# Two-layer diffusion backbone: the first two projection items of a chunk issued in turns, and the second layer's modulation moved to later items

## The chip, the cores and the metric

One NeuronCore of one Trainium2 chip. The metric is the device time of one execution in microseconds; three runs of the kernel before are shown by their median. One profiled execution is read in detail. The engines are TensorE (PE, its weight loads PEld), VectorE (DVE), ScalarE (ACT), GpSimd (POOL) and SyncE (SP), which here issues the DMA transfers.

## The reference

Two layers, each: RMS norm with a modulation computed from a condition vector, one input projection whose columns feed three mixers (latent attention, grouped attention, a convolution module), a gate on each, one output projection, and a residual.

```python
shift, scale, gate = split(silu(c) @ w_mod + b_mod, 3)
h = rms_norm(x, norm_w) * (1 + scale) + shift
p = h @ w_in                               # 2048 tokens x 1024, and 256 context tokens likewise
y = concat([o_mla, o_gqa, o_conv]) * silu(p[..., OFF_GATE:])
x_new = x + gate * (y @ w_out)
```

After the second layer comes a final RMS norm. Everything is float32.

## The kernel before, in words

The kernel alternates three calls of `projections(l)` (l = 0 and 1 for the layers, 2 for the end stage, which has the last output projection only) with two calls of `attention`. The change lies in `projections`.

**The work of a projection stage** is a list of *items* (L517 on): one weight tile of 128 output columns times one chunk of tokens. Chunks 0 to 3 have 512 tokens, chunk 4 is the context with 256. Kind "o" is the output projection of the layer before, kind "i" the input projection; the first layer has 105 items, the second 128, the end stage 32. An item takes 24 matmuls: for each of 8 slices k of the contraction the three products wh·xh, wh·xl and wl·xh, since weight and operand are each split into a rounded part (h) and a remainder (l). They add up in one PSUM bank of `mm` (two banks; three in the end stage).

**Weights.** `w_loads` brings raw tiles into two buffers `wraw`; `w_splits` turns raw weight j into `wset[j % 2]`, ACT rounding it to wh and POOL subtracting to wl. It may do so only after the last item that uses weight j − 2 (the `after(("item", w_last[j - 2]))` in it).

**Operands.** `x_prep(c)` makes chunk c's operands for kind "i", slice by slice: DVE scales a loaded tile of x by the modulation and the norm's bank, ACT adds the shift and rounds into xh, DVE subtracts into xl; then slice k counts as there. They stand in `big`: chunks 0 and 2 in `big2`, chunks 1 and 3 in `big0`, the context in `big1`. `y_k` does the like for kind "o". `stats` computes a chunk's norm, `post` and `out_post` take an item's result out of PSUM, `mod_part(m, part, start)` computes a part of layer m's modulation: w_mod tiles of 256 KB, in groups of four matmuls that run side by side in four strips of the array, and then transposes. It waits for item `start` to begin (`at(start)` looks at `at_item`).

**What sets the order.** A planner in the kernel, which runs when it is built: `Sched` holds generators with priorities, `Clock` a model of when each engine is free and each tile readable, and `Sched.run` lets the generators issue whatever the model holds ready. Each engine then carries out its instructions in the order in which they were issued. `mains` (L585), with priority 9, issues the items one after another: per slice it yields until the weights and the slice are ready, and after every second slice it yields once more. So whatever changes in the pace of `mains` changes the order on DVE, ACT, POOL and SP as well.

Of the kernel before, what the change touches and what calls it, by code (L numbers as in the profile page):

```python
# [22 lines left out]
CH = [(0, 512), (512, 512), (1024, 512), (1536, 512), (2048, 256)]  # L23
EPS = 1e-6
KD = D // 128
# [22 lines left out]
INF = float("inf")  # L48
# [240 lines left out]
def hybrid_dit(ctx: ExitStack, tc: tile.TileContext, I: dict, out: bass.AP):  # L289
    nc = tc.nc  # L290
    clk = Clock()
    V, A, G, T = (Engine(clk, n, e) for n, e in
                  (("DVE", nc.vector), ("ACT", nc.scalar), ("POOL", nc.gpsimd), ("PE", nc.tensor)))
# [37 lines left out]
    wset = [[const.tile([128, KD, 128], F32R, name=f"w{s}{i}") for s in "hl"] for i in range(2)]  # L331
# [96 lines left out]
    def q_parts(z, u, q):  # L428

        h, c = u  # L430
        W = CH[c][1]
        if h < MH:
# [6 lines left out]
        for e in (0, 64):  # L439
            parts += [(q[i][e:e + 64, 0:W], n[i]) for i in range(2)]  # L440
            if h < MH:
                parts += [(q[2][e + 32 * i:e + 32 * i + 32, 0:W], src[i, 64:96, :]) for i in range(2)]
                parts.append((q[3][e:e + 32, 0:W], src[0, 64:96, :]))
        return [(o.bitcast(F32), i) for o, i in parts]

    def m_parts(u, q, row):
        W = CH[u[1]][1]
        return [(q[3][e:e + 1, 0:W].bitcast(F32), row.unsqueeze(0)) for e in (32, 96)]

    def projections(l):  # L450
# [5 lines left out]
        sch = Sched(clk, S)  # L456
        load, store = sch.load, sch.store
        done = set()
        at_item = [0]
        open_ = [True]  # L460

        def after(what):
            return lambda: 0.0 if what in done else INF

        def at(n):
            return lambda: 0.0 if at_item[0] >= n else INF
# [35 lines left out]
        items = []  # L502
# [21 lines left out]
        w_last, x_first, x_last = {}, {}, {}  # L524
# [49 lines left out]
        def operand(who):  # L574
            t = big[hold[who]]
            if who[1] == 4:
                t = t[:, 0].rearrange("p (s k) (e w) -> p s (k e) w", s=2, e=2)
            return t[:, 0], t[:, 1]

        def freed(who):  # L580
            if before[who] is None:
                return after("S1") if who == ("o", 1) else None
            return after(("item", before[who]))

        def mains():  # L585
            for n, (j, c, kind, what) in enumerate(items):
                at_item[0] = n
                W = CH[c][1]
                ps = yield from mm.take()
                if kind == "o":  # L590
                    sch.add(0, out_post(n, c, what, ps[:, 0:W]))
                wh, wl = wset[j % 2]
                yield after(("w", j))
                xh, xl = operand((kind, c))
                ops = ((wh, xh), (wh, xl)) if what == "kr" else ((wh, xh), (wh, xl), (wl, xh))
                i = 0
                for k in range(KD):
                    yield [wh, wl, after((kind, c, k))]
                    for a, b in ops:
                        T.matmul(out=ps[:, 0:W], lhsT=a[:, k, :], rhs=b[:, k, 0:W],  # L600
                                 start=(i == 0), stop=(i == len(ops) * KD - 1))
                        i += 1
                    if k % 2:
                        yield
                done.add(("item", n))
                if kind == "i":
                    sch.add(0, post(what, c, ps[:, 0:W]))
            at_item[0] = len(items)
            open_[0] = False

# [678 lines left out]
        def rest_y():  # L1289
            yield from all_y([(c, k) for c in ochunks[2:] for k in range(KD)])  # L1290
            open_lanes[0] = False
# [13 lines left out]
        with ExitStack() as es:  # L1305
            wk = es.enter_context(tc.tile_pool(name=f"wk{l}", bufs=1, reuse_waits="tile"))
            pb = es.enter_context(tc.tile_pool(name=f"pb{l}", bufs=1, space=PSUM, reuse_waits="tile"))
            new = [wk.tile([128, 512], F32, name=f"sb{l}_{i}") for i in range(NSLOT + (10 if end else 0))]
            if first:
                sb = Slots(clk, lent)  # L1310
            sb.extend(new)
            sr = Slots(clk, [] if end else [big[1][:, 1, k, :] for k in range(1, KD)]
                       + [wk.tile([128, 512], F32R, name=f"sr{l}_{i}") for i in range(NSLOTR)])
            wn = Slots(clk, [wk.tile([128, 512 + 2 * HALO], F32, name=f"wn{l}_{i}") for i in range(0 if end else 2)])
            mm = Slots(clk, [pb.tile([128, 512], F32, name=f"mm{l}_{i}") for i in range(3 if end else NMM)])
            aux = Slots(clk, [pb.tile([128, 512], F32, name=f"aux{l}_{i}") for i in range(5 if end else 8 - NMM)])
            if not end:
                sw = es.enter_context(tc.tile_pool(name=f"sw{l}", bufs=1, reuse_waits="tile"))
                p = pars[l]
                qn, kvn, gkn, dww, dwb, lnw, lnb, pwb = p.qn, p.kvn, p.gkn, p.dww, p.dwb, p.lnw, p.lnb, p.pwb  # L1320
                gqs = p.gqn
                V.tensor_scalar(out=gqs, in0=p.gqn, scalar1=0.125, scalar2=None, op0=ALU.mult)
                uv_h = sw.tile([128, 384], F32R, name=f"uv_h{l}")
                uv_l = sw.tile([128, 384], F32R, name=f"uv_l{l}")

            sch.add(9, mains())
            if first:
                sch.add(1, w_loads())
                sch.add(1, w_splits())
            else:  # L1330
                sch.add(2, rest_y())
                for _ in range(LANES_P):
                    sch.add(2, runner(lanes, open_lanes))
            if not end:
                if first:
                    sch.add(2, stats(0, True, None))
                    sch.add(2, mod_part(0, 0, 0))
                    sch.add(3, stats(1, KEEP1, after(("raw", 1)) if AFTW else after("w_mod")))
                    sch.add(3, stats(4, False, at(1)))
                    sch.add(3, stats(2, False, at(20)))  # L1340
                    sch.add(3, stats(3, False, at(30)))
                    sch.add(6, mod_part(0, 1, 14), 2000)
                    sch.add(6, mod_part(1, 0, 50), 2000)
                    sch.add(6, mod_part(1, 1, 70), 2000)
                for c in (0, 1, 4, 2, 3):
                    sch.add(2, x_prep(c))
                sch.add(6, small_weights(n_out + 2), 3000)
                sch.add(3, runner(heavy, open_), 6000)
                for _ in range(2):
                    sch.add(4, runner(light, open_), 5000)  # L1350
                for _ in range(2):
                    sch.add(5, conv_run(), CLIM)
                sch.add(5, first_unit(), 6000)
            sch.run()
# [405 lines left out]
```

## Time and profile before

| | us |
|---|---|
| median of 3 runs | 3965.18 (3965.15 to 3965.5) |
| profiled execution | 3964.66 |
| its span, first to last instruction | 3962.8 |
| PE busy | 3838.4 (97%) |
| DVE, POOL, ACT busy | 2699.1, 2487.7, 1869.5 |

The profile's times count from the start of the span; all steps run through helpers on line L160, so that tiles, not lines, tell the work apart. PE busy is the time with at least one matmul under way; the granted clock is TensorE's, 1.00 for full speed, and a matmul at 0.50 takes twice as long.

### The profile page before, as it was taken

What the parts mean: (1) busy time and instruction counts of PE and PEld (TensorE: products, weight loads), DVE (VectorE), ACT (ScalarE), POOL (GpSimd) and SP (SyncE); (2) the same over time, 40 slices, a digit from 0 to 9 for tenths busy, and PEclk for the clock granted to TensorE, in tenths of its full rate; (3) what the DMA queues carried; (4) which work ended last, traced back from release to release, by engine and by line L of the source; (5) the groups of instructions that cost most, each with busy time, mean ns of one, the idle gap of its engine ahead of it and who ended that gap; (6) DMA issues with size and microseconds to landing.
All of it is one profiled execution on the core that took longest, in us unless ns stands there. A gap on an engine that the chain in (4) does not pass through costs nothing. (4 is left out here: it accounts for less than half of the span.)

```text
span 3962.8 us, 60573 instructions
## 1 busy us (share of the span) xinstructions
PE 3838.4 (97%) x22674; PEld 2645.0 (67%) x22674; DVE 2699.1 (68%) x4017; ACT 1869.5 (47%) x2461; POOL 2487.7 (63%) x1277
## 2 busy tenths in 40 slices
PE   7999999899999999999999999999999999999998
PEld 4888677555556666665778887775655666666576
DVE  5545379688888776677434645887888877666743
ACT  5555376444444444444435645654444444444442
POOL 3452164377777777778445424547888788888844
PEclk9999999899999999999999999999999999999999
DMA  6456654411212332212654463543121133222264
GB/s 214 159 174 200 193 164 148 109 36 37 61 36 65 88 77 66 70 55 79 233 180 136 159 200 126 182 137 75 37 59 28 48 78 77 64 63 69 79 216 148
DMA packets 314712, 438.44 MB, mean 111 GB/s; under 512 B 78625, under 2 KB 149102, under 8 KB 314418
## 3 DMA queue, kind: packets, MB, share of 16 engines
q1 hardware_dynamic: 314418, 434.56, 36.9%
q8 instruction: 179, 2.93, 0.3%
q14 instruction: 115, 0.94, 0.1%
HBM read 304.94 MB, written 121.07 MB: 108 GB/s over the span
## 5 line engine op out<-in xcount | busy, mean ns | idle before, releaser
L160 PE MATMUL mm<-big,wh 128*128 128x512 f32 (+1 forms) x4240 | 1282.6, 388 | 34.1 <-DVE big L160 18.0
L160 POOL TENSOR_TENSOR acc<-acc,p 128x1024 f32<-128x1024 f32 x478 | 1174.2, 2456 | 207.5 <-DVE p L160 130.4
L160 DVE TENSOR_REDUCE mx<-m 128x1 f32<-128x512 f32 (+2 forms) x1716 | 1079.1, 680 | 223.4 <-PE m L160 216.1
L160 ACT ACTIVATE p<-s 128x1024 f32<-128x1024 f32 (+1 forms) x682 | 695.0, 1020 | 746.3 <-PE s L160 701.0
L160 PEld LDWEIGHTS mm<-big,wh 128*128 128x128 f32 x4240 | 782.7, 190 | 234.7 <-issue 53.7
L160 PE MATMUL s<-qh,big 64*128 64x512 f32 (+1 forms) x3504 | 794.4, 408 | 1.0 <-DVE n L160 0.4
L160 PE MATMUL mm<-big,wl 128*128 128x512 f32 (+1 forms) x2040 | 775.8, 380 | 2.9 <-POOL wl L160 2.9
L160 POOL TENSOR_TENSOR wl<-wraw,wh 128x1024 fp32r<-128x1024 f32 x132 | 317.9, 2410 | 614.9 <-ACT wh L160 581.1
L160 PE MATMUL o<-p,big 128*64 128x512 f32 (+1 forms) x2728 | 655.8, 599 | 3.3 <-DVE n L160 3.1
L160 PE MATMUL m<-big,qh 64*128 64x512 f32 (+1 forms) x2304 | 476.1, 360 | 32.7 <-DVE mx L160 24.0
L160 PEld LDWEIGHTS s<-qh,big 64*128 64x128 f32 x3504 | 401.9, 186 | 135.2 <-issue 88.1
L160 PEld LDWEIGHTS mm<-big,wl 128*128 128x128 f32 x2040 | 388.2, 190 | 76.1 <-POOL wl L160 4.6
L160 PEld LDWEIGHTS o<-p,big 128*64 128x64 f32 x2728 | 188.9, 138 | 361.5 <-issue 350.1
L160 PE MATMUL s<-ql,big 64*128 64x512 f32 (+1 forms) x1752 | 390.8, 390 | 0.0
L160 POOL TENSOR_TENSOR acc<-acc,wraw 128x1024 f32<-128x1024 f32 x142 | 346.3, 2439 | 48.7 <-DVE wraw L160 32.9
L160 PEld LDWEIGHTS m<-big,qh 64*128 64x128 f32 x2304 | 298.4, 188 | 113.8 <-DVE mx L160 64.5
L160 DVE SCALAR_TENSOR_TENSOR aux<-wn,par,aux 128x512 f32<-128x512 f32 (+1 forms) x396 | 259.7, 718 | 99.7 <-ACT aux L160 63.8
L160 POOL TENSOR_TENSOR sb<-sb,sb 128x512 f32<-128x512 f32 (+2 forms) x151 | 182.8, 1220 | 204.6 <-ACT sb L160 160.3
L160 ACT ACTIVATE wraw<-s 128x1024 f32<-128x1024 f32 (+1 forms) x194 | 198.2, 1022 | 175.5 <-PE s L160 163.9
L160 DVE SCALAR_TENSOR_TENSOR aux<-aux,sb 128x512 f32<-128x512 f32 (+1 forms) x198 | 129.4, 654 | 147.8 <-ACT sb L160 143.1
L160 PEld LDWEIGHTS s<-ql,big 64*128 64x128 f32 x1752 | 207.9, 187 | 14.7
L160 PE MATMUL s<-qd,zm 33*128 33x512 f32 (+1 forms) x876 | 208.0, 396 | 7.4 <-DMA qd<-nm 7.4
(176 smaller groups left out, 4795.6 us busy)
## 6 DMA issues: line engine op xcount, KB each, us to landing
wraw<-in_w_in SPq DMA_DIRECT2D x84, 512.0 KB
wraw<-in_w_out SPq DMA_DIRECT2D x48, 512.0 KB
sb<-in_w_mod SPq DMA_DIRECT2D x75, 256.0 KB
sb<-in_x SPq DMA_DIRECT2D x60, 256.0 KB
gt<-sb SPq DMA_DIRECT2D x57, 256.0 KB
big<-kn SPq DMA_DIRECT2D x48, 288.0 KB
sb<-x SPq DMA_DIRECT2D x53, 256.0 KB
qh<-qg SPq DMA_DIRECT2D x96, 128.0 KB
```

The source lines that it names most:

```text
L160: return f(**kw)
```

## The change

`mains` now takes its items from a generator `item(n)`, whose body is unchanged. Where item n is the first of its kind and chunk, and item n + 1 has the same kind, both are added as tasks of their own with priority 9, so that the planner takes them in turns, and `mains` waits for both. In addition layer 2's modulation starts at item 68 instead of 50 (32 w_mod tiles) and at item 80 instead of 70 (16 tiles).

```diff
+        def item(n):
+            j, c, kind, what = items[n]
+            at_item[0] = n
...
         def mains():
-            for n, (j, c, kind, what) in enumerate(items):
-                at_item[0] = n
...
+            n = 0
+            while n < len(items):
+                _, c, kind, _ = items[n]
+                if x_first[kind, c] == n and n + 1 < len(items) and items[n + 1][2] == kind:
+                    left = [2]
+
+                    def lane(i, left):
+                        yield from item(i)
+                        left[0] -= 1
+
+                    sch.add(9, lane(n, left))
+                    sch.add(9, lane(n + 1, left))
+                    yield lambda: INF if left[0] else 0.0
+                    n += 2
+                else:
+                    yield from item(n)
+                    n += 1
...
-                    sch.add(6, mod_part(1, 0, 50), 2000)
-                    sch.add(6, mod_part(1, 1, 70), 2000)
+                    sch.add(6, mod_part(1, 0, 68), 2000)
+                    sch.add(6, mod_part(1, 1, 80), 2000)
```

What this does to the order of the instructions, at three places. In the names, the digits right after `mm`, `big`, `wh` and `wl` tell banks and buffers apart.

PE, second layer, around the border of items 0 and 1 and up to item 2 (banks mm1_0 and mm1_1, weights 0, 1 and then 2, which takes the place of 0). Before, the last slice of item 0 and the first two of item 1:

```order
L160 MATMUL mm1_0_17313<-big0_72,wh0_93 128x512 x2
L160 MATMUL mm1_0_17313<-big0_72,wl0_94 128x512
L160 MATMUL mm1_1_17314<-big0_72,wh1_95 128x512 x2
L160 MATMUL mm1_1_17314<-big0_72,wl1_96 128x512
L160 MATMUL mm1_1_17314<-big0_72,wh1_95 128x512 x2
L160 MATMUL mm1_1_17314<-big0_72,wl1_96 128x512
```

Now, the last slice of item 0, the last two of item 1, and the first of item 2:

```order
L160 MATMUL mm1_0_17313<-big0_72,wh0_93 128x512 x2
L160 MATMUL mm1_0_17313<-big0_72,wl0_94 128x512
L160 MATMUL mm1_1_17314<-big0_72,wh1_95 128x512 x2
L160 MATMUL mm1_1_17314<-big0_72,wl1_96 128x512
L160 MATMUL mm1_1_17314<-big0_72,wh1_95 128x512 x2
L160 MATMUL mm1_1_17314<-big0_72,wl1_96 128x512
L160 MATMUL mm1_0_17313<-big0_72,wh0_93 128x512 x2
L160 MATMUL mm1_0_17313<-big0_72,wl0_94 128x512
```

Two slices of one item follow two of the other, to the end. Between the last matmul of item 0 and item 2 there stand now 6 matmuls of item 1, where there were 24.

DVE, second layer, chunks 2 and 3 (big2 is chunk 2, big0 chunk 3; `sb<-sb,ascale` scales a tile, `big<-...,mod,big` is the subtraction into xl; chunk 3's bank of the norm is aux1_1 before and aux1_2 now). Before, from the scaling of chunk 3 on to chunk 2's last subtractions:

```order
L160 SCALAR_TENSOR_TENSOR sb1_4_17292<-sb1_4_17292,ascale1_104,aux1_1_17316 128x512
L160 SCALAR_TENSOR_TENSOR sb1_2_17290<-sb1_2_17290,ascale1_104,aux1_1_17316 128x512
L160 SCALAR_TENSOR_TENSOR sb1_0_17288<-sb1_0_17288,ascale1_104,aux1_1_17316 128x512
L160 SCALAR_TENSOR_TENSOR lent0_97<-lent0_97,ascale1_104,aux1_2_17317 128x512
L160 SCALAR_TENSOR_TENSOR big2_74<-lent3_100,mod1_102,big2_74 128x512
L160 SCALAR_TENSOR_TENSOR sb1_9_17297<-sb1_9_17297,ascale1_104,aux1_2_17317 128x512
L160 SCALAR_TENSOR_TENSOR big2_74<-sb1_6_17294,mod1_102,big2_74 128x512
L160 SCALAR_TENSOR_TENSOR sb1_3_17291<-sb1_3_17291,ascale1_104,aux1_1_17316 128x512
L160 TENSOR_TENSOR big1_73<-aux1_4_17319,big1_73 128x512
L160 SCALAR_TENSOR_TENSOR big2_74<-lent0_97,mod1_102,big2_74 128x512
L160 SCALAR_TENSOR_TENSOR sb1_5_17293<-sb1_5_17293,ascale1_104,aux1_1_17316 128x512
L160 SCALAR_TENSOR_TENSOR big2_74<-sb1_9_17297,mod1_102,big2_74 128x512
```

Now, the last rows of the same piece of work:

```order
L160 TENSOR_TENSOR aux1_4_17319<-aux1_4_17319,lent2_99 128x512
L160 SCALAR_TENSOR_TENSOR sb1_14_17302<-sb1_14_17302,ascale1_104,aux1_2_17317 128x512
L160 SCALAR_TENSOR_TENSOR big0_72<-lent0_97,mod1_102,big0_72 128x512
L160 SCALAR_TENSOR_TENSOR sb1_5_17293<-sb1_5_17293,ascale1_104,aux1_2_17317 128x512
L160 SCALAR_TENSOR_TENSOR big0_72<-sb1_1_17289,mod1_102,big0_72 128x512
L160 SCALAR_TENSOR_TENSOR big0_72<-sb1_14_17302,mod1_102,big0_72 128x512
L160 SCALAR_TENSOR_TENSOR big0_72<-sb1_5_17293,mod1_102,big0_72 128x512
L160 SCALAR_TENSOR_TENSOR sb1_3_17291<-sb1_3_17291,ascale1_104,aux1_1_17316 128x512
L160 SCALAR_TENSOR_TENSOR big2_74<-sb1_2_17290,mod1_102,big2_74 128x512
L160 SCALAR_TENSOR_TENSOR big2_74<-sb1_0_17288,mod1_102,big2_74 128x512
L160 TENSOR_TENSOR sr1_0_17304<-aux1_4_17319,sr1_4_17308 128x512
L160 SCALAR_TENSOR_TENSOR big2_74<-sb1_3_17291,mod1_102,big2_74 128x512
```

Chunk 2's subtractions for k4 to k7 stood ahead of all of chunk 3's; now its last three stand behind all eight of chunk 3's.

DVE, first layer, chunks 2 and 3, between chunk 2's subtractions for k4 and k5. Before, from k4 to k6:

```order
L160 SCALAR_TENSOR_TENSOR big2_74<-lent1_98,mod0_101,big2_74 128x512
L160 SCALAR_TENSOR_TENSOR sb0_15_432<-sb0_15_432,ascale0_103,aux0_3_447 128x512
L160 SCALAR_TENSOR_TENSOR sb0_14_431<-sb0_14_431,ascale0_103,aux0_3_447 128x512
L160 SCALAR_TENSOR_TENSOR big0_72<-lent2_99,mod0_101,big0_72 128x512
L160 SCALAR_TENSOR_TENSOR big0_72<-sb0_5_422,mod0_101,big0_72 128x512
L160 SCALAR_TENSOR_TENSOR big0_72<-sb0_13_430,mod0_101,big0_72 128x512
L160 SCALAR_TENSOR_TENSOR lent3_100<-lent3_100,ascale0_103,aux0_0_444 128x512
L160 SCALAR_TENSOR_TENSOR big2_74<-sb0_0_417,mod0_101,big2_74 128x512
L160 SCALAR_TENSOR_TENSOR big2_74<-sb0_1_418,mod0_101,big2_74 128x512
```

Now, up to k5 (k4 stands three rows above the first):

```order
L160 SCALAR_TENSOR_TENSOR sb0_0_417<-sb0_0_417,ascale0_103,aux0_5_449 128x512
L160 TENSOR_TENSOR big1_73<-aux0_1_445,sr0_2_435 128x512
L160 TENSOR_TENSOR sr0_3_436<-aux0_4_448,big1_73 128x512
L160 SCALAR_TENSOR_TENSOR sb0_7_424<-sb0_7_424,ascale0_103,aux0_5_449 128x512
L160 SCALAR_TENSOR_TENSOR sb0_2_419<-sb0_2_419,ascale0_103,aux0_5_449 128x512
L160 SCALAR_TENSOR_TENSOR big0_72<-sb0_6_423,mod0_101,big0_72 128x512
L160 SCALAR_TENSOR_TENSOR big0_72<-sb0_9_426,mod0_101,big0_72 128x512
L160 SCALAR_TENSOR_TENSOR big0_72<-sb0_0_417,mod0_101,big0_72 128x512
L160 SCALAR_TENSOR_TENSOR aux0_0_444<-aux0_0_444,sb0_13_430 128x256 x3
L160 SCALAR_TENSOR_TENSOR aux0_0_444<-sb0_12_429,par_105,aux0_0_444 128x256
L160 SCALAR_TENSOR_TENSOR sb0_8_425<-sb0_8_425,ascale0_103,aux0_2_446 128x512
L160 SCALAR_TENSOR_TENSOR big2_74<-lent3_100,mod0_101,big2_74 128x512
```

Between the two stood six rows and now stand thirteen, among them five of chunk 3's scalings and a chain of the convolution.

## Rows read from the trace of the kernel before

**Rows 1.** the page: the span, then the busy time, share and instructions of each engine, then the largest group of section 5 (busy us, mean ns of one | idle before, and its releaser).

```profile
span 3962.8 us, 60573 instructions
...
PE 3838.4 (97%) x22674; PEld 2645.0 (67%) x22674; DVE 2699.1 (68%) x4017; ACT 1869.5 (47%) x2461; POOL 2487.7 (63%) x1277
...
L160 PE MATMUL mm<-big,wh 128*128 128x512 f32 (+1 forms) x4240 | 1282.6, 388 | 34.1 <-DVE big L160 18.0
```

**Rows 2.** the windows: stretch, its length, then busy us (and instructions) of PE, PEld, DVE, ACT and POOL, the granted clock of TensorE, the DMA share and GB/s. In order: the modulation loads of the opening, a stretch after one weight wait, chunks 2 and 3 of the first layer, attention, chunks 2 and 3 of the second layer, and a part of that.

```profile
5.00:40.00 35.00, 23.94 (x71) 5.25 (x71) 11.16 (x18) 11.71 (x19) 4.08 (x2) 0.91 1.03 374
...
97.00:100.20 3.20, 0.93 (x4) 0.40 (x3) 0.00 (x0) 1.48 (x3) 3.20 (x3) 1.00 0.00 0
...
410.00:456.00 46.00, 37.80 (x155) 22.94 (x155) 21.83 (x36) 16.18 (x27) 6.98 (x5) 0.85 0.69 226
...
1000.00:1050.00 50.00, 48.58 (x320) 27.16 (x319) 44.74 (x63) 21.54 (x23) 39.87 (x17) 1.00 0.46 86
...
2382.00:2411.00 29.00, 25.77 (x99) 19.80 (x98) 17.67 (x26) 14.18 (x22) 6.08 (x3) 0.88 0.44 152
...
2388.80:2395.40 6.60, 6.10 (x13) 4.14 (x14) 5.91 (x10) 3.31 (x7) 0.00 (x0) 0.50 0.70 251
```

**Rows 3.** the table of waits: engine, line, what it waited for, us in total, times, longest us.

```profile
PE mm L160 <- DVE big L160: 18.0, 18, 4.0
```

**Rows 4.** the timeline, PE and POOL, in the opening of the first layer (start us, length us, engine, line, operation, tiles, count, and in brackets the idle time before it and who ended it; all timelines below are read so).

```profile
39.96 0.79 PE L160 MATMUL mm<-big,wh 128*128 128x512 f32 x1 [4.36 <-ACT big L160]
...
47.80 0.50 PE L160 MATMUL mm<-big,wh 128*128 128x512 f32 x1 [0.35 <-DVE big L160]
...
49.52 0.39 PE L160 MATMUL mm<-big,wl 128*128 128x512 f32 x1
...
51.63 2.41 POOL L160 TENSOR_TENSOR wl<-wraw,wh 128x1024 fp32r<-128x1024 f32 x1 [11.04 <-ACT wh L160]
...
54.97 0.39 PE L160 MATMUL mm<-big,wl 128*128 128x512 f32 x1
...
100.10 0.50 PE L160 MATMUL mm<-big,wl 128*128 128x512 f32 x1 [2.05 <-POOL wl L160]
```

**Rows 5.** the timeline, PE, ACT and POOL, in the second layer's items 0 to 2.

```profile
1896.45 0.39 PE L160 MATMUL mm<-big,wl 128*128 128x512 f32 x1
...
1896.65 1.06 ACT L160 ACTIVATE wh<-wraw 128x1024 fp32r<-128x1024 f32 x1 [14.82 <-PE mm L160]
...
1896.68 0.62 PE L160 MATMUL mm<-big,wh 128*128 128x512 f32 x2
...
1897.79 2.40 POOL L160 TENSOR_TENSOR wl<-wraw,wh 128x1024 fp32r<-128x1024 f32 x1 [16.08 <-ACT wh L160]
...
1902.12 0.62 PE L160 MATMUL mm<-big,wh 128*128 128x512 f32 x2
...
1902.57 0.39 PE L160 MATMUL mm<-big,wl 128*128 128x512 f32 x1
```

**Rows 6.** the timeline of PE in chunk 2 and 3 of the first layer: the first matmul of item 63, the waits in it, a modulation group, and the first matmul of item 67.

```profile
410.28 0.63 PE L160 MATMUL mm<-big,wh 128*128 128x512 f32 x2
...
419.88 0.79 PE L160 MATMUL mm<-big,wh 128*128 128x512 f32 x1 [4.04 <-DVE big L160]
...
422.30 2.58 PE L160 MATMUL aux<-sb,sc 128*32 128x512 f32 x5 [1.20 <-DMA sb<-in_w_mod]
...
428.71 0.50 PE L160 MATMUL mm<-big,wh 128*128 128x512 f32 x1 [2.03 <-DVE big L160]
...
431.96 0.79 PE L160 MATMUL mm<-big,wh 128*128 128x512 f32 x1 [0.92 <-DVE big L160]
...
450.69 1.07 PE L160 MATMUL aux<-sb,sc 128*32 128x512 f32 x8
...
455.01 0.62 PE L160 MATMUL mm<-big,wh 128*128 128x512 f32 x2
```

**Rows 7.** the timeline of PE in the second layer's context chunk.

```profile
2042.62 0.58 PE L160 MATMUL mm<-big,wh 128*128 128x256 f32 x1 [2.98 <-DVE big L160]
...
2049.90 0.50 PE L160 MATMUL mm<-big,wl 128*128 128x512 f32 x1 [0.26 <-POOL wl L160]
```

**Rows 8.** the timeline, PE and DVE, in chunk 2 of the second layer: item 86's first matmul, DVE's scaling of chunk 3, the waits of PE, DVE's subtraction for k7, the last matmul of item 87 and the first of item 90.

```profile
2382.00 0.62 PE L160 MATMUL mm<-big,wh 128*128 128x512 f32 x2
...
2384.27 2.06 DVE L160 SCALAR_TENSOR_TENSOR sb<-sb,ascale,aux 128x512 f32<-128x512 f32 x3 [1.73 <-ACT aux L160]
...
2387.71 0.50 PE L160 MATMUL mm<-big,wh 128*128 128x512 f32 x1 [2.60 <-DVE big L160]
...
2389.03 0.79 PE L160 MATMUL mm<-big,wh 128*128 128x512 f32 x1 [0.36 <-DVE big L160]
...
2390.95 0.80 PE L160 MATMUL mm<-big,wh 128*128 128x512 f32 x1 [0.27 <-DVE big L160]
...
2391.47 0.75 DVE L160 SCALAR_TENSOR_TENSOR big<-sb,mod,big 128x512 fp32r<-128x512 f32 x1
...
2399.58 0.39 PE L160 MATMUL mm<-big,wl 128*128 128x512 f32 x1
...
2410.68 0.62 PE L160 MATMUL mm<-big,wh 128*128 128x512 f32 x2
```

**Rows 9.** the timeline of PE where the first layer's attention begins.

```profile
740.84 0.79 PE L160 MATMUL s<-qd,zm 33*128 33x512 f32 x1 [5.62 <-DMA qd<-nm]
```

More of the change, by code (lines that the diff above doesn't have):

```diff
@@ L583, in freed @@
             return after(("item", before[who]))
-        def mains():
-            for n, (j, c, kind, what) in enumerate(items):
-                at_item[0] = n
[L588 to L607, printed above, removed]
+        def item(n):
+            j, c, kind, what = items[n]
+            at_item[0] = n
+            W = CH[c][1]
+            ps = yield from mm.take()
+            if kind == "o":
+                sch.add(0, out_post(n, c, what, ps[:, 0:W]))
+            wh, wl = wset[j % 2]
+            yield after(("w", j))
+            xh, xl = operand((kind, c))
+            ops = ((wh, xh), (wh, xl)) if what == "kr" else ((wh, xh), (wh, xl), (wl, xh))
+            i = 0
+            for k in range(KD):
+                yield [wh, wl, after((kind, c, k))]
+                for a, b in ops:
+                    T.matmul(out=ps[:, 0:W], lhsT=a[:, k, :], rhs=b[:, k, 0:W],
+                             start=(i == 0), stop=(i == len(ops) * KD - 1))
+                    i += 1
+                if k % 2:
+                    yield
+            done.add(("item", n))
+            if kind == "i":
+                sch.add(0, post(what, c, ps[:, 0:W]))
```

## The prediction, made before the changed kernel ran

> **What bounds the kernel now.** I read the page first. TensorE (PE) is busy 3838.4 of 3962.8 us, and the projection matmuls mm<-big,wh are its largest group [rows 1]. So the time is PE's, and a change of order can only move the 124 us in which PE is idle and the stretches in which its matmuls take twice as long. The windows come next: in attention PE is busy 48.58 of 50 us at a granted clock of 1.00, while in the first layer's stretch of chunks 2 and 3 it is 37.80 of 46 us at 0.85, and in the second layer's 25.77 of 29 us at 0.88 [rows 2]. The table of waits names the cause: PE waited 18.0 us in 18 places for big written by DVE, the operands of a new chunk [rows 3]. Last come the timelines of those places [rows 4 to 8], to see for each pair of items which operand arrives last, and what is queued on DVE ahead of it.
>
> Two prices recur. A 512-column matmul takes 0.227 us at full clock (24 of them from 1896.68 to 1902.12 [rows 5]), so an item of 24 is 5.44 us, and twice that at a granted clock of 0.50. A DVE step of x_prep on 512 columns takes 0.66 us back to back (2.06 us for three, overlapping a little [rows 8]). After a wait of 2.60 us the clock was 0.50 from 2388.8 to 2395.4; after one of 2.05 us at 100.10 it stayed at 1.00 [rows 2, 4, 8]. A drop of that length costs up to 3.3 us, less where operands are late anyway.
>
> **The change, part by part.** No matmul, DVE or POOL work and no transfer is added; the order on every engine of the three projection stages changes. In attention PE's order is the same, so I cost it at nothing: there is no new instruction there to pay for.
>
> 1. *Opening of the first layer.* The second lane of the pair sets at_item to 1 at once, so four ctx tiles (512 KB together) now go ahead of the last w_mod load in a stretch whose DMA share is 1.03 at 374 GB/s [rows 2]: +1.4 us on the start of item 0, at 39.96 before. The operands of k4 to k7, which came with 0.35 us of wait each (the last at 47.80 [rows 4]), now meet two items' work, so the pair of 48 matmuls ends near 54.6, 0.8 us sooner than item 1 did (55.36 [rows 4]). But weight 2 may be split only after item 0's last matmul, which moves from 49.91 [rows 4] to about 53.2: its wl was ready at 54.04 [rows 4] and is now at about 58, 3 us after item 2 wants it. Chunk 1 then starts some 2 us later, pair 4/5 wins 2.7 by filling operand waits, and both orders meet at the wl that let PE go at 100.10 [rows 4], which depends on POOL's queue. Net +0.4. Bounds: −3 (both pairs win, wl comes sooner) and +5 (the 3 us stay, with a drop of the clock).
>
> 2. *First layer, chunks 2 and 3.* Before, items 63 to 66 take 410.28 to 455.01, 44.7 us [rows 6], for 96 matmuls (21.8 us) and five modulation groups of about 1.0 us (1.07 with the overlap at its end, at 450.69 [rows 6]) with their transposes, 0.4. The rest is waits of 4.04, 1.20, 2.03 and 0.92 us [rows 6] and half clock. Now no modulation group stands in this stretch; its 5.4 us are paid later, where PE has no gap to hide them. But DVE's new order holds 16 instructions from chunk 2's k4 to its k5 (three steps of a chain count as three), and another 5 to k7. With k4 at about 415.7, k5 comes at 415.7 + 16 × 0.66 = 426.3; PE has done ten products' worth (k0 to k4 of both items, 30 × 0.227 = 6.8 us) by 417.1 and waits 9 us. Then 18 matmuls, mostly at half clock (7.4 us), and 48 of chunk 3 (10.9): item 67 at 444.6 instead of 455.01, −10.4; with the 5.4 moved, **−5.0**. Bounds: −13 (k5 to k7 in time) and +2 (a second drop and the x loads late, as their queue also carries the blocking raw weights).
>
> 3. *End of the first layer.* The last modulation part and the column sums of the last convolution now stand behind item 104, beside a wait of 5.62 us for a transfer at 740.84 [rows 9] that decides when attention starts. A few DVE and PE steps more ahead of it: +0.6, between −4 and +4 by that wait.
>
> 4. *Second layer, items 0 and 1.* Before, item 0 ended at 1896.84; ACT rounded weight 2 from 1896.65, POOL had its wl at 1900.19, and item 2's first wl product ran at 1902.57 [rows 5], 2.4 us of slack. In a pair of 6 and 6 matmuls, item 0 ends 1.36 us (six matmuls) before the pair does, at 1900.9, so wl is ready 4.1 us later, at 1904.3, and PE stands at 1902.57 waiting for it: **+1.7**. Nothing else can fill this, because item 2's third matmul holds PE. The end stage's first pair has the same shape: **+1.7**. Bounds for each: +1, +5 with a drop of the clock.
>
> 5. *Second layer, context chunk.* Its last three subtractions stand four to six DVE rows later than before, behind those of chunk 1. Before, PE waited 2.98 us for them at 2042.62, and 0.26 us for a wl at 2049.90 [rows 7]. Six rows are 4 us, of which the wl wait and the pairing give back about 1.5: **+2.5**, bounds 0 and +6.
>
> 6. *Second layer, chunks 2 and 3, the largest term.* Before, k4 to k6 reached PE at 2387.71, 2389.03 and 2390.95, with waits of 2.60, 0.36 and 0.27, and k7's subtraction ran at 2391.47 [rows 8]; items 86 to 89 took from 2382.00 to 2410.68, 28.7 us for 21.8 us of matmuls. In the new DVE order chunk 3's tiles are scaled from the row that answers to 2384.27 on, and chunk 2's k4, k5 and k7 are the 14th, 25th and 28th instruction from there. At 0.66 us: k4 at 2393.5, k5 at 2400.8, k7 at 2402.8. PE has the rest done in 6.8 us and stands twice, about 4 and 6 us. Its matmuls go in program order, so chunk 3, though ready, cannot pass chunk 2. The last 18 matmuls of the pair run mostly at 0.50 (7.4 us, to 2408.2), chunk 3's 48 take 10.9: item 90 at 2419.1 instead of 2410.68, **+8.4**. Bounds: +2 (DVE starts the stretch 2.4 us sooner and the clock holds) and +11 (2.2 us more, where a step waits for a rope swap behind a blocked weight load).
>
> Sum: 0.4 − 5.0 + 0.6 + 1.7 + 2.5 + 8.4 + 1.7 = **+10.3 us**, on the profiled 3964.66 us gives 3975.0. The median shown, 3965.18, is 0.5 above that execution, so 3975.5.
>
> The alternation itself I cost at nothing: in attention PE turns between its s, m and o banks, 320 matmuls in 50 us, at a granted clock of 1.00 [rows 2]. The Trainium skill, "TensorE: Matmul & The Clock Gate", section "A second HAM failure mode: psum-queue depth-cycling", speaks against the change: it reports a kernel that cycled through PSUM banks and whose clock went up and down between its groups. By that rule the time would be rival D's, by the row it is the sum's, and the row shows no such drop.
>
> **Rivals.**
> A. *Chunk 2's operands come in time in the second layer.* Place: 2382 to 2411. If k5 reaches PE by about 2389 to 2391, as before, the pair does what its interleaving suggests: it ends near 2393.5 instead of 2399.97, about −6 in place of +8.4. Sum −4.1, time 3961. For it: the waits there were only 3.2 us before [rows 8]. Against: DVE's 25 instructions, which are fixed. It decides from k5 before 2391 on; on this side the kernel is not slower. Chance 0.25.
> B. *A, and chunk 2 of the first layer too*, since the modulation loads no longer share the DMA with x there: −13 in place of −5.0. Sum −12, time 3953. Against it stands the same kind of DVE order. Chance 0.20.
> C. *The change does little of what it says.* Several pairs (items 6/7 of the first layer, 24/25 of the second) are emitted as 24 and 24 anyway, and if the weights' splits and late operands take exactly what pairing gives, the time stays at 3966. Chance 0.03.
> D. *Alternating between two PSUM banks costs clock.* Some 300 matmuls in the interleaved pairs at half clock would add 300 × 0.227 = 68 us, 4043. Against it stands attention's 1.00 [rows 2]. Chance 0.02.
> The forecast keeps 0.50.
>
> **How the numbers follow.** About 0.2%, 7.9 us, is what a measurement of this kernel can tell from no change: below 3957.3 is faster, above 3973.1 slower. The forecast's own bounds run from 3966 (term 6 at +2, term 5 at 0) to 3989 (terms 4 and 6 at their upper ends). It gives 0.48 of its 0.50 to slower, D adds 0.02, and the small bounds of terms 1 and 3 leave a little: slower 0.52. A and C, less what lies beyond, make same 0.28; B faster 0.20. The range from 3956 to 3989 leaves out the better part of B, D, and the drops that come on top of one another.
>
> **What would show it.** PE's timeline: items 0 and 1 of each stage take turns, and item 2's first wl product waits 1.5 to 2 us for POOL in the second layer and the end stage. In the second layer's chunk 2 PE waits for DVE's big before k4 and before k5, 4 to 6 us each, at a granted clock near 0.5 after, and item 90 starts 37 us after item 86 did, not 28.7. In the first layer items 63 to 66 take about 34 us, with one wait near 9. I should be wrong if chunk 2's operands come within 1 us of one another there, or if the table of waits names a transfer instead of DVE.

## The result, and the profile after

The changed kernel takes 3984.99 us (median of 6 runs, 3983.79 to 3987.43), the kernel before 3965.28 beside it (6 runs, 3963.41 to 3966.25): a ratio of 1.0050, with a 95% interval of 1.0039 to 1.0060. It is **slower by 19.7 us, 0.5%**. The forecast had the sign, and 3984.99 lies in its range of 3956 to 3989; the sum, +10.3, is half of what came. The profiled spans differ by 3982.0 − 3962.8 = 19.2 us, and the steps below are read against that. In experiment 5 below one run of nine took 4586.89 us at a mean granted clock of 0.78, and its figures leave that run out.

The page of after, in the rows that answer to [rows 1]:

```profile
span 3982.0 us, 60569 instructions
...
PE 3839.8 (96%) x22674; PEld 2641.1 (66%) x22674; DVE 2694.2 (68%) x4017; ACT 1846.7 (46%) x2444; POOL 2485.0 (62%) x1277
...
L160 PE MATMUL mm<-big,wh 128*128 128x512 f32 (+1 forms) x4240 | 1282.3, 388 | 48.8 <-DVE big L160 26.9
```

PE does the same work in the same busy time (3839.8 against 3838.4). What grew is the idle time ahead of the projection matmuls: from 34.1 to 48.8 us ahead of those with wh, and from 2.9 to 11.6 ahead of those with wl. The waits that grew, in the table of waits of after (columns as in [rows 3], which held 18 waits):

```profile
PE mm L160 <- DVE big L160: 26.9, 12, 8.6
...
PE mm L160 <- ACT big L160: 11.7, 5, 4.3
PE mm L160 <- POOL wl L160: 11.5, 11, 1.8
```

Fewer waits for DVE's operands, but longer ones; five for ACT's, where before had 3 and 10.6 us; and eleven for a weight's remainder, 11.5 us, where before had 3 of them and 2.9 us.

Where the time went is best seen at the starts of items, taken from the first matmul of each in program order. Each column is the difference from before; the last two are experiments described below. A column is read from one trace, and within a trace short stretches are steady: in six traces that share their first layer (experiments 2 and 8 to 12) items 63 to 67 take between 23.38 and 23.42 us.

| start of | before, us | after | modulation alone | pairs alone |
|---|---|---|---|---|
| first layer, item 63 | 410.28 | +2.3 | −3.3 | +11.5 |
| item 67 | 455.01 | −7.7 | −24.6 | −0.4 |
| second layer, item 0 | 1888.77 | −6.3 | −12.1 | +3.0 |
| item 86 | 2382.00 | −0.3 | −12.1 | +11.3 |
| item 90 | 2410.68 | +10.2 | −12.1 | +21.4 |
| end stage, item 0 | 3768.76 | +11.2 | −12.6 | +23.7 |
| item 10 | 3825.31 | +17.0 | −13.7 | +30.1 |
| item 31 | 3941.33 | +18.3 | −13.7 | +31.4 |

*The second layer's chunk 2*, PE, then DVE, then SP, where [rows 8] stood before:

```profile
2381.71 0.62 PE L160 MATMUL mm<-big,wh 128*128 128x512 f32 x2
...
2396.50 0.80 PE L160 MATMUL mm<-big,wh 128*128 128x512 f32 x1 [6.95 <-DVE big L160]
...
2403.71 0.80 PE L160 MATMUL mm<-big,wh 128*128 128x512 f32 x1 [4.28 <-DVE big L160]
...
2420.85 0.61 PE L160 MATMUL mm<-big,wh 128*128 128x512 f32 x2
2422.39 0.50 PE L160 MATMUL mm<-big,wl 128*128 128x512 f32 x1 [0.93 <-POOL wl L160]
```

```profile
2387.10 0.75 DVE L160 SCALAR_TENSOR_TENSOR big<-lent,mod,big 128x512 fp32r<-128x512 f32 x1
2390.48 0.70 DVE L160 TENSOR_TENSOR aux<-aux,sb 128x512 f32<-128x512 f32 x1 [2.63 <-issue]
...
2395.70 0.74 DVE L160 SCALAR_TENSOR_TENSOR big<-sb,mod,big 128x512 fp32r<-128x512 f32 x1
...
2402.91 1.41 DVE L160 SCALAR_TENSOR_TENSOR big<-sb,mod,big 128x512 fp32r<-128x512 f32 x2
```

```profile
2381.20 0.32 SPq L245 DMA_DIRECT2D gt<-sb  x1
2385.28 0.33 SPq L245 DMA_DIRECT2D wraw<-in_w_in  x1
...
2386.14 0.51 SPq L245 DMA_DIRECT2D sb<-sb  x1
```

PE stands twice, before k4 and before k5, as forecast, and each wait ends with the DVE subtraction in the second fence (k4's starts at 2395.70, k5's at 2402.91). Item 90 starts 39.1 us after item 86. Besides the queued instructions DVE lost 2.63 us ahead of 2390.48, a sum of the rope that reads the tile brought by the swap transfer sb<-sb. SP issued that at 2386.14, after it had stood at a raw weight load from 2381.52 to 2385.28. The granted clock after k4's wait (the windows, columns as in [rows 2]):

```profile
2395.00:2410.00 15.00, 9.21 (x24) 6.58 (x25) 10.58 (x17) 5.17 (x9) 0.00 (x0) 0.57 0.21 70
```

*The first layer's chunks 2 and 3* in after, for [rows 6]: one wait for operands, of 8.62, and no modulation.

```profile
429.71 0.79 PE L160 MATMUL mm<-big,wh 128*128 128x512 f32 x1 [8.62 <-DVE big L160]
```

*The end of the first layer*, for [rows 9]: the first matmul that reads the transferred tile runs within half a us of its time in before (740.84), but PE no longer waits ahead of it, and the clock holds. The windows after it are of before, from that matmul to 765, and of after, from the same matmul to the same matmul:

```profile
740.30 0.40 PE L160 MATMUL s<-qd,zm 33*128 33x512 f32 x1
```

```profile
740.84:765.00 24.16, 18.68 (x74) 11.40 (x76) 15.57 (x27) 8.02 (x8) 11.84 (x9) 0.50 0.89 191
```

```profile
740.30:754.50 14.20, 12.59 (x76) 7.07 (x75) 12.90 (x23) 7.42 (x7) 10.46 (x7) 1.00 1.14 217
```

What before did in 24.2 us at a granted clock of 0.50, after does in 14.2 at 1.00. By 779 us, where before has come back to full clock as well, about 11 us are won at one place.

*The first pairs of the second layer and of the end stage*: PE, then POOL in the first; ACT, PE and POOL in the second ([rows 5] before).

```profile
1895.30 0.70 PE L160 MATMUL mm<-big,wh 128*128 128x512 f32 x2 [0.18 <-DVE sb L160]
1897.26 0.50 PE L160 MATMUL mm<-big,wl 128*128 128x512 f32 x1 [1.25 <-POOL wl L160]
...
1894.83 4.73 POOL L160 TENSOR_TENSOR wl<-wraw,wh 128x1024 fp32r<-128x1024 f32 x2 [20.29 <-ACT wh L160]
```

```profile
3792.55 0.60 ACT L160 ACTIVATE aux<-big 128x512 f32<-128x512 f32 x1 [1.52 <-DMA big<-o]
3793.08 1.99 ACT L160 ACTIVATE wh<-wraw 128x1024 fp32r<-128x1024 f32 x2
...
3794.18 0.73 PE L160 MATMUL mm<-big,wh 128*128 128x512 f32 x2 [1.38 <-ACT wh L160]
3796.62 0.50 PE L160 MATMUL mm<-big,wl 128*128 128x512 f32 x1 [1.71 <-POOL wl L160]
3796.95 0.88 PE L160 MATMUL mm<-big,wh 128*128 128x512 f32 x2
...
3794.20 4.71 POOL L160 TENSOR_TENSOR wl<-wraw,wh 128x1024 fp32r<-128x1024 f32 x2 [22.78 <-ACT wh L160]
```

In the end stage item 0's last matmul ended at 3791.4. ACT could have rounded weight 2 then, but at the head of its queue stood a copy of a tile of the gathered o (aux<-big), which waited for its transfer until 3792.55. PE waits for the rounding and then for the remainder, and its matmuls go on at half clock (two in 0.88 us and 1.05, not 0.62).

### The profile page after: what moved, and what is told of

It is laid out like the page before. It is cut to its first block, busy times and chain, and to the rows that moved or that the text cites. A ratio compares the mean times of both kernels' runs of the same rounds, so it can differ in the third digit from the quotient of the medians.

```text
span 3982.0 us, 60569 instructions
## 1 busy us (share of the span) xinstructions
PE 3839.8 (96%) x22674; PEld 2641.1 (66%) x22674; DVE 2694.2 (68%) x4017; ACT 1846.7 (46%) x2444; POOL 2485.0 (62%) x1277
## 3 DMA queue, kind: packets, MB, share of 16 engines
q8 instruction: 179, 2.93, 0.3%
## 5 line engine op out<-in xcount | busy, mean ns | idle before, releaser
L160 PE MATMUL mm<-big,wh 128*128 128x512 f32 (+1 forms) x4240 | 1282.3, 388 | 48.8 <-DVE big L160 26.9
L160 PE MATMUL mm<-big,wl 128*128 128x512 f32 (+1 forms) x2040 | 777.2, 381 | 11.6 <-POOL wl L160 11.5
L160 POOL TENSOR_TENSOR sb<-sb,sb 128x512 f32<-128x512 f32 (+2 forms) x164 | 196.2, 1205 | 138.9 <-ACT sb L160 118.6
L160 PE MATMUL o<-wraw,big 128*64 128x512 f32 x776 | 206.2, 594 | 0.1
```

The source lines that it names most:

```text
L160: return f(**kw)
```

## The experiments

**1 and 2, the two parts of the change apart.** The pairs with the modulation's old start:

```diff
-                    sch.add(6, mod_part(1, 0, 68), 2000)
-                    sch.add(6, mod_part(1, 1, 80), 2000)
+                    sch.add(6, mod_part(1, 0, 50), 2000)
+                    sch.add(6, mod_part(1, 1, 70), 2000)
```

> Pairs as in the change, the second layer's modulation again from items 50 and 70. Theory M (what the first layer's chunks 2 and 3 gain comes from the modulation leaving that stretch): the stretch from item 63's first matmul to item 67's, 44.7 us before and 34.7 in the change, is back near 45 us, and the time is 3988 to 3992. Theory P (the pairs give it): the stretch stays below 40 us, time 3983 to 3986.

The kernel before with the new starts, 68 and 80 (the same two lines the other way):

> No pairs; the second layer's modulation from items 68 and 80. Theory M: the stretch from item 63 to 67 falls from 44.7 to 34 to 37 us, some 5 us of modulation matmuls are paid later, time 3957 to 3962. Theory P: the stretch keeps over 40 us, time 3963 to 3967. The rest of the change's loss (19 to 20 us) is then all the pairs' in either case.

Measured: pairs alone 3996.36 (3993.46 to 3998.33), ratio 1.0075 [1.0062, 1.0088]; modulation alone **3954.15** (3951.60 to 3959.84), ratio 0.9971 [0.9960, 0.9981], faster than both kernels. At the end of the table above the two add up: 31.4 − 13.7 = 17.7, and after stands at 18.3. So the change is a gain of some 13 us and a loss of some 31. Place by place they don't: each part alone makes the stretch from item 63 to item 67 shorter, and both together are no better there than the pairs alone. Neither theory of experiment 1 held whole: its stretch fell as under P, its time lay above both. Experiment 2 went further than M said. In the stretch from item 63 to item 67, 44.7 us before, the modulation alone leaves

```profile
407.01:430.40 23.39, 22.79 (x104) 18.66 (x103) 16.35 (x20) 11.79 (x19) 7.72 (x4) 1.00 0.47 144
```

that is 23.4 us at full clock, in which PE waits once, 0.60 us for a remainder; with the pairs alone it is 32.8, with both 34.7. Much of the gain ends at a transfer: 24.6 us ahead at item 67, PE waits longer where attention begins.

```profile
729.85 0.79 PE L160 MATMUL s<-qd,zm 33*128 33x512 f32 x1 [12.13 <-DMA qd<-nm]
```

**3, 4 and 5, why the second layer's chunk 2 is late.** First, no pairs for chunks 2 and 3 there:

```diff
-                if x_first[kind, c] == n and n + 1 < len(items) and items[n + 1][2] == kind:
+                if x_first[kind, c] == n and n + 1 < len(items) and items[n + 1][2] == kind and (l, kind, c) not in ((1, "i", 2), (1, "i", 3)):
```

> The change without its two pairs in the second layer's chunks 2 and 3 (items 86 to 89 one after the other again). Theory D (the late operands there, 6.95 and 4.28 us of waits, come from the order that the pair brought to DVE): item 86 to item 90 takes 28 to 30 us as before instead of 39.1, time 3973 to 3976. Rival T (transfers are late there in this order of the whole stage anyway): over 34 us, time over 3980.

Measured 3984.58, ratio 1.0048 [1.0034, 1.0062], and from item 86 to 90 41.3 us, not fewer: PE waited 3.94, 6.01 and 5.56 us. The pair there is not what makes DVE take chunk 3 first; it even saves about 2 us.

Then chunk 3's scaling held back until chunk 2 is done, in `x_prep`:

```diff
+            if l == 1 and c == 3:
+                yield after(("i", 2, KD - 1))
```

> The change with the pairs kept, but in the second layer chunk 3's scaling begins only when chunk 2's last slice has been issued, so that DVE has chunk 2's k3 to k7 ahead of all of chunk 3. Theory D: k7 reaches PE by 2393 instead of 2405, chunk 3's pair then runs at DVE's pace, item 86 to 90 takes 25 to 30 us, time 3971 to 3976. Rival A (the alternation of items on PE, or the loads, cost it): still over 35 us, time over 3981.

Measured 3980.46 (3977.68 to 3983.16), ratio 1.0036 [1.0023, 1.0049]; items 86 to 90 in 34.7 us, so 4.5 of the 10.5 lost are back, fewer than expected. PE, SP and DVE show the rest:

```profile
2395.32 0.80 PE L160 MATMUL mm<-big,wh 128*128 128x512 f32 x1 [5.52 <-DVE big L160]
...
2382.21 0.32 SPq L245 DMA_DIRECT2D gt<-sb  x1
2386.30 0.33 SPq L245 DMA_DIRECT2D wraw<-in_w_in  x1
...
2387.16 0.51 SPq L245 DMA_DIRECT2D sb<-sb  x1
...
2391.90 0.70 DVE L160 TENSOR_TENSOR aux<-aux,sb 128x512 f32<-128x512 f32 x1 [9.84 <-issue]
```

DVE now stands for 9.84 us at the same rope sum, whose swapped tile SP did not fetch while the weight load stood at the head of its queue (that the sum waited for this transfer is read from the names of its tiles; the trace gives no releaser). Third, no pair of kind "i" anywhere in the second layer, the same condition with `(l, kind) != (1, "i")` in effect:

> The change without any of the second layer's pairs of kind i (items 40/41, 42/43, 50/51, 86/87, 88/89); its o pairs stay. Leaving out 86 to 89 alone had changed nothing, since DVE kept chunk 3 ahead. Theory E (the earlier pairs of the same stage set that order): DVE has chunk 2 ahead of chunk 3 again, item 86 to 90 takes 28 to 30 us instead of 39.1, time 3972 to 3976. Rival T (transfers and queues of this stage are late in any case once the o pairs stand): over 34 us, time over 3980.

Measured 3972.8 (3969.34 to 3982.16), ratio 1.0024 [1.0014, 1.0034]; items 86 to 90 in 27.9 us (before 28.7), and the waits are of before's size:

```profile
2392.60 0.80 PE L160 MATMUL mm<-big,wh 128*128 128x512 f32 x1 [2.60 <-DVE big L160]
2395.84 0.80 PE L160 MATMUL mm<-big,wh 128*128 128x512 f32 x1 [0.27 <-DVE big L160]
```

Experiments 3 and 5 differ only in the earlier pairs of kind "i" of this stage (chunks 0, 1 and the context), so these bring the order that makes chunk 2 late; that they do it through the planner's clock is argued, and which of them, no run tells. The pairs of kind "o" aren't needed for it: experiment 7 leaves them out, and items 86 to 90 still take 40.2 us.

**6, at_item.** The second lane does not raise `at_item` until the pair is done, so that prefetches start when they did before:

```diff
-        def item(n):
+        def item(n, second=False):
...
-            at_item[0] = n
+            if not second:
+                at_item[0] = n
```

> The change, but the second lane of a pair no longer raises at_item; it rises when the pair is done. Theory I (the early rise alone brings the context loads forward and with them the DVE order of the first layer's chunks 2 and 3): item 0 starts at 40 to 41 us instead of 43.6, items 63 to 67 take 23 to 27 us instead of 34.7 (DVE has chunk 2 ahead of chunk 3 there), time 3971 to 3976. Rival W (it costs only the loads' own 1.4 us and the planner's order is due to the pairs): 32 us and more, time 3981 to 3985.

Measured 3986.29, ratio 1.0062 [1.0048, 1.0076]. The mechanism is there: item 0 starts at 41.4 us instead of 43.6, and items 63 to 67 take 24.6. Yet the 22.0 us won at item 67 are 8.0 at item 104 and 7.5 where the second layer begins (after: 6.3): PE then waits near the layer's end for POOL and ACT,

```profile
728.18 2.07 PE L160 MATMUL aux<-sb,ones_f 128*128 128x512 f32 x2 [3.38 <-POOL sb L160]
736.80 0.80 PE L160 MATMUL aux<-sr,qh 128*128 128x512 f32 x1 [6.54 <-ACT sr L160]
```

and the first layer's last chain, not its projections, decides when attention starts.

**7, no pairs of kind "o"** (the condition with `and kind == "i"`):

> The change without the pairs of kind o (second layer items 0/1, 8/9, 24/25, 26/27; end stage 0/1, 8/9, 24/25). Theory S (the weight split that a pair leaves uncovered is what the o pairs cost): the waits for POOL's wl before item 2 and the 2.0 us before item 10 go, item 2 of the end stage takes 5.6 us instead of 9.3; 10 to 13 us less, time 3972 to 3975. Rival C (the waits only change place, into the operands of item 0 and of chunk 1 as before): under 5 us less, time over 3980.

Measured 3966.88 (3965.01 to 3970.86), ratio 1.0006 [0.9997, 1.0015]: 18 us better than after, more than expected. By the starts of items it is 16.2 us ahead of after at the last one: 2.2 from before the second layer, 4.2 from that layer's items 0 to 10, which lose nothing here, 3.4 from items 26 to 51, and 8.1 in the end stage, whose items 0 to 10 win 1.1 here and lose 5.8 in after; 1.8 go the other way from item 86 to the end stage. Pairs at one place seem to reach others through the planner's order.

**8, the modulation and one pair**, that of the second layer's chunk 2 (condition `and (l, kind, c) in ((1, "i", 2),)`):

> The later modulation with one pair alone, items 86/87 of the second layer, where DVE has chunk 2 ahead of chunk 3 as before. Theory G (a pair gains where its operands come one by one and its next weight is not late): the waits of 2.60, 0.36 and 0.27 us there and the half clock after them go, item 86 to 90 takes 22 to 25 us instead of 28.7, time 3947 to 3951 beside the 3954 of the later modulation alone. Rival N (what the pair gains it loses on a weight split or on chunk 3's operands): 27 to 30 us, time 3953 to 3956.

Measured 3951.84 (3948.93 to 3955.74), ratio 0.9968 [0.9955, 0.9980]. The pair wins 2.6 us by item 88, and chunk 3's operands, now wanted sooner, cost 1.85 of them by item 90. The 0.8 that stays can't be told from experiment 2 by the times, whose intervals lie over one another.

**9 to 12, one pair in the end stage**, on the kernel of experiment 2. Here the stretch from item 0 to 10 of that stage tells the cost, 55.5 us without a pair; totals also hold differences of up to 5 us in the first layer's end, which all four share in program and not in time (last section). First the plain pair (`and (l, kind, c) == (2, "o", 0)`):

> The later modulation with one pair alone, items 0 and 1 of the end stage. All operands of that chunk are there when it begins, so the pair has nothing to gain. Theory S (the weight split that the pair leaves with six matmuls of cover, and ACT's queue ahead of it, cost the end stage's 5.8 us): item 2's first and third matmul wait for ACT and POOL, 2 to 3.5 us together, its matmuls then run partly at half clock; from item 0's start to item 10's start 61 to 63 us instead of 55.5 (later modulation alone), time 3958 to 3962 beside 3954. Rival O (that loss comes from orders set by other pairs): 55 to 57 us, time 3952 to 3956.

Measured 3963.24, ratio 0.9991 [0.9982, 1.0000]; items 0 to 10 in 63.7 us. Item 0 ended at 3765.6, and ACT came to weight 2 only at 3769.15:

```profile
3768.62 0.60 ACT L160 ACTIVATE aux<-big 128x512 f32<-128x512 f32 x1 [1.75 <-DMA big<-o]
3769.15 1.99 ACT L160 ACTIVATE wh<-wraw 128x1024 fp32r<-128x1024 f32 x2
```

Then the second lane starts six slices after the first, so that 18 matmuls, 4.1 us, cover the split:

```diff
+                if k == 5:
+                    done.add(("lead", n))
...
+                        if lead:
+                            yield after(("lead", i - 1))
```

> The same single pair, but the second lane begins only after six slices of the first, so that 18 matmuls (4.1 us) instead of 6 stand between item 0's last and item 2. Theory S: the split of about 3.6 us is covered, no wait of over 0.3 us for POOL or ACT, item 0 to 10 takes 55 to 56.5 us, time 3952 to 3956. Rival O or alternation itself: as with the even pair.

Measured 3960.46, ratio 0.9982 [0.9971, 0.9994]; 61.9 us. Item 0 ended at 3764.4, but ACT stood at two tiles of other work:

```profile
3766.75 0.60 ACT L160 ACTIVATE aux<-big 128x512 f32<-128x512 f32 x1 [12.51 <-DMA big<-o]
3768.83 0.63 ACT L160 ACTIVATE sb<-sb 128x512 f32<-128x512 f32 x1 [1.48 <-DVE sb L160]
3769.36 1.04 ACT L160 ACTIVATE wh<-wraw 128x1024 fp32r<-128x1024 f32 x1
```

Cover alone does not help when the split itself is queued. Next the plain pair, with ACT's copies for the next chunk and its squares of the stage's results held until weight 2 is split:

```diff
+                if end:
+                    yield after(("w", 2))
                 yield t
...
             mm.give(ps)
+            if end:
+                yield after(("w", 2))
```

> As the single even pair of the end stage, but ACT's copies for the next chunk and its squares of item 0's result wait until weight 2 is split, so that the rounding of weight 2 is ACT's first step after item 0's last matmul. Theory Q (the led pair did not help because the rounding stood 3.5 to 5 us behind ACT steps that wait for transfers and for DVE; the missing cover of the split is a smaller part): no wait for ACT, a wait of 1.7 us for POOL's wl is left, item 0 to 10 takes 57 to 59 us instead of 63. Rival V (the alternation or the late transfers cost it): over 61 us.

Measured 3963.09, ratio 0.9985 [0.9976, 0.9994]; 58.9 us, with one wait left. The first line is near item 0's start, the second item 2's wait, at a clock that holds:

```profile
3767.61 0.63 PE L160 MATMUL mm<-big,wl 128*128 128x512 f32 x1
...
3780.45 0.50 PE L160 MATMUL mm<-big,wl 128*128 128x512 f32 x1 [1.57 <-POOL wl L160]
```

Last both edits together:

> The same with the led pair, 18 matmuls (4.1 us) between item 0's last and item 2. Theory Q: both parts are covered, no wait of over 0.3 us at item 2, item 0 to 10 takes 55 to 56.5 us, as with the later modulation alone (55.5), time 3952 to 3957. Rival V: over 59 us.

Measured 3958.27, ratio 0.9978 [0.9969, 0.9987]; 57.1 us, no wait at item 2, and what is left above 55.5 lies before item 2. There PE doesn't wait either; in experiments 11 and 12 the first 3 us or so after item 0's start run at half clock (the first line above: 0.63 us, not 0.39), and in 2, 9 and 10 they don't. Before, which has no pair, shows such a stretch at the same place, so it isn't the pair's. What decides it, no run tells: the wait with which attention ends is alike in all five experiments, 1.83 to 2.11 us. From item 0 to item 2 it costs 1.6 us in each of the two experiments. Without it the four come out at 8.2, 6.4, 1.8 and 0 us above 55.5: of the plain pair's 8.2 us, 6.4 came from ACT's queue and 1.8 from the missing cover. The pair wins nothing even so: without it PE waits for no operand of these items.

## Why the prediction was right, and where its sum was not

Each term beside the difference between the two profiles, from the starts of items:

| term | forecast | measured |
|---|---|---|
| 1 opening, to item 63 | +0.4 | +2.3 |
| 2 items 63 to 67 | −10.4 | −10.0 |
| 2, 3 item 67 to the second layer (modulation, end) | +6.0 | +1.3 |
| 4 second layer, items 0 to 8 | +1.7 | +1.5 |
| items 8 to 26 | 0 | +2.3 |
| 5 context chunk, items 26 to 51 | +2.5 | +3.1 |
| items 51 to 86 | 0 | −0.8 |
| 6 items 86 to 90 | +8.4 | +10.5 |
| item 90 to the end stage | 0 | +1.1 |
| 4 end stage, items 0 to 10 | +1.7 | +5.8 |
| end stage, items 10 to 31 | 0 | +1.3 |

The measured column ends at item 31 and adds up to 18.3; the last 1.0 of the 19.2 us lies behind it.

**Right:** the largest term. k4 was forecast at 2393.5 and came at 2396.5, k5 at 2400.8 and came at 2403.7; the count of DVE's queue gave the 7.3 us between them, and the start of the chain slipped by 2.63 us at the rope, which the upper bound of term 6 had named and priced at 2.2. The first layer's wait was forecast near 9 and measured 8.62. Item 2's wait for POOL in the second layer is there. Rival A, operands in time, is refuted by the two waits, rival B with it, and rival C by the interval. Rival D: items 88 and 89, which take turns of 6 to 12 matmuls between two banks, ran at full clock. The Trainium skill ("TensorE: Matmul & The Clock Gate", section "A second HAM failure mode: psum-queue depth-cycling") reports a clock that goes up and down where PE idles briefly between groups that cycle through banks. The trace doesn't show that here, with PE busy for all of these 8 us:

```profile
2412.00:2420.00 8.00, 8.00 (x37) 6.63 (x36) 0.00 (x0) 1.55 (x2) 1.19 (x2) 1.00 0.10 35
```

**Mis-sized, the end stage's half of term 4:** it was taken to be the second layer's pair again, with weight 2 split as soon as item 0 ends. ACT's place in its own queue was not looked up: there the rounding stood behind a copy that waited for a transfer, and half clock followed the waits. Predicted +1.7, measured +5.8, and experiments 9 to 12 show both parts, the queue and the cover. **Left out,** items 8 and 9 of the second layer, a pair as well, of chunks 1 and 2 with one weight, costed at nothing (+2.2, with a wait of 2.00 us ahead of item 10 at 1943.86; the profile names ACT's big, but item 10 reads operands that item 8 had read, and more likely it waited for DVE, which emptied a bank (sb<-mm) until 1943.71), and +1.3 in the end stage behind item 26, with a wait of 0.99 us for POOL's wl at 3932.74. Experiment 7, without the pairs of kind "o", shows neither; which of these pairs brings the second, no run tells.

**Term 3 was mis-sized the other way.** I took the wait of 5.62 us for granted and did not see that the half clock after it lasted 24 us. After's PE comes late enough not to wait, and wins 11 there, far outside the term's bounds of −4 and +4. The +1.3 in the table hides this: items 67 to 104 lose 8.6 us, where 5.4 stood; 1.5 come back by the start of attention and the 11 right behind it; and the rest of attention, costed at nothing, loses 5.5, of which 3.7 at one place (last section). So that the time lies in the range is in part luck: without those 11 us it would be near 3996. And the upper end of the range isn't the sum that the prediction gives for it: terms 4 and 6 at their upper ends add 9.2 to 3975.5, which is 3984.7 and not 3989. The stretch 97.00 to 100.20 of [rows 2], read as the clock after a wait, ends with that wait; from 100.10 to 106 the granted clock was 1.00 too, so that reading stands. **A cause left open:** term 6 took the DVE order as it stood and didn't ask which pair makes it. Experiments 3 and 5 show that earlier pairs do, and not the one that waits. For the time it made no difference, since the order was read off and not inferred. And the modulation alone was worth 13 us; term 2 costs it together with the pairs at −5.0, and the forecast never took the two parts of the change apart.

## What to carry to other kernels

Before two items are put side by side, look up who frees their buffers: ending both late delays the next weight's split, and that split then stands in ACT's queue behind whatever else is there. Here moving side work away from late operands won 13 us, and filling the waits with a second item lost 31; such parts are worth trying one by one. When an order changes on an in-order queue, price the waits at the head (a raw weight load on SP, a copy waiting for a gather on ACT), not only the number of instructions ahead.

## What the runs showed of the hardware that was not expected

The same two DVE additions in attention took 2.90 us in before's trace and 5.09 to 5.12 in that of every changed kernel. PE waits for what is behind them. Before, then after; the two rows behind the first mark are the second addition and the POOL addition that runs beside it:

```profile
1392.40 2.90 DVE L160 TENSOR_TENSOR big<-lent,big 128x512 fp32r<-128x512 f32 x2
...
1394.62 0.68 DVE L160 TENSOR_TENSOR big<-lent,big 128x512 fp32r<-128x512 f32 x1
1394.61 2.93 POOL L160 TENSOR_TENSOR acc<-acc,p 128x1024 f32<-128x1024 f32 x1 [0.47 <-ACT p L160]
```

```profile
1380.52 5.11 DVE L160 TENSOR_TENSOR big<-lent,big 128x512 fp32r<-128x512 f32 x2
...
1382.79 2.83 DVE L160 TENSOR_TENSOR big<-lent,big 128x512 fp32r<-128x512 f32 x1
1382.72 2.35 POOL L160 TENSOR_TENSOR acc<-acc,p 128x1024 f32<-128x1024 f32 x1 [0.41 <-ACT p L160]
...
1386.28 0.49 PE L160 MATMUL m<-big,qh 64*128 64x512 f32 x1 [3.00 <-DVE mx L160]
...
1386.00:1391.00 5.00, 4.72 (x28) 3.75 (x30) 3.40 (x6) 1.02 (x1) 2.83 (x2) 0.66 0.44 124
```

It costs 3.7 us with the lower clock after it. The traces show what goes with it. In after the second addition starts 0.07 us behind POOL's and takes 2.83 us; in before the two start within 0.01 us of one another, DVE's takes 0.68 and POOL's is the longer one, 2.93 in place of 2.35. Of the 518 DVE steps of this form (TENSOR_TENSOR, 128x512) in each trace, those with no POOL instruction beside them took 0.67 to 0.70 us (206 in before, 233 in after), and all that took over 0.76, up to 2.89 (99 and 97), had one. Steps that read a PSUM bank kept their time beside POOL: 55 of aux<-aux,sb in before, at most 0.70. So the two engines hold each other up here, and some hundredths of a us decide which one pays; the kernel's planner reckons with it (`Clock.issue` lets POOL and a DVE step that reads no PSUM take turns). No run moved one against the other, so this is read from the traces and not shown by an experiment.

And one program's first layer is not equally long each time: experiments 2 and 8 to 12 have the same one, reach item 104 between 18.3 and 19.9 us ahead of before, and begin the second layer between 7.3 and 12.8 ahead.
